# A hybrid SSD and pooling layer: the output projection as seven block products over all 16 k tiles, and the plain form of the seven in the down projection

## The chip, the cores and the metric

The kernel runs on one core of a Trainium2 chip. The metric is the device time of one execution in microseconds (us), given as the median of several runs; one execution of it is recorded by the profiler. Engines: PE multiplies matrices (PEld loads its weights), DVE and ACT work on vectors, POOL is the GpSimd engine, and SP issues DMAs. Each engine takes its own instructions in the order in which they stand in its queue. POOL and ACT issue DMAs too, and such an issue stands in their queues as an instruction.

## The reference

One decoder layer over 1024 prompt tokens and 8 sample tokens (1032 columns), all in float32. What matters here:

```
hn   = rmsnorm(x, norm1_w)
proj = hn @ w_in                          # z, xBC, dt, v
y_ssd, y_pool = ssd(...), pool_mixer(v)   # 1536 + 512 channels
x  = x + concat([y_ssd, y_pool]) @ w_out  # 2048 -> 1024
hn = rmsnorm(x, norm2_w)
u  = causal_dwconv(hn @ w_up)             # 1024 -> 2 * 2816
x  = x + (silu(gate) * val) @ w_down      # 2816 -> 1024
y  = rmsnorm(x, final_norm_w)
```

The states of the convolutions, the scan and the pooling are outputs as well; the change does not touch them.

## The kernel before

All activations lie feature-major: a k tile is 128 features by 1032 tokens. To keep float32 accuracy, every operand is split into a high part (ACT copies it to a shorter float type) and a low part (DVE subtracts that copy from the original): `split` does it for the moving operands (lines 208 to 212), `weight_parts` for weights of up to 512 columns (134 to 142). A product of two tiles is then three matmuls (high x high, high x low, low x high) which add up in PSUM.

The program's stages in the recorded execution: input projection, scan and pooling end at 516 us, the output projection `w_out` runs to 717.7, the up projection to 1165, the down projection and the final norm to the end at 1406.

**The output projection** (`w_out`, line 894). Two parts of six SSD tiles each run over the eight outputs n in chunks of 344 tokens, 18 matmuls a chunk; DVE adds each chunk from PSUM onto the residual `x2` (line 920). The four pooling tiles come last, one half of the tokens after the other, in columns of 258 (`w_out_end`, line 956); their evacuations (line 969) complete an output, ACT squares it (976), POOL or a product with ones adds the squares up, and `rn` gives the norm of the up projection's input. Weights come by SP straight from DRAM, in pieces of 384 or 512 columns. The last pooling group (`pool_tile`, line 834) ends beside the first SSD rows: its window sums on DVE and POOL, a split, nine products with the weights `pw`, and an evacuation to `pf`.

Twelve times in `w_out`, `down_sums` (line 1240) is called. It loads four blocks of the down weights, forms their sums for four of the seven products of the down projection with POOL, and puts them into DRAM.

**The down projection** (`down`, line 1305). The matrix product is cut into 2 x 2 blocks (even and odd output tiles by two halves of the 22 k tiles; two halves of 516 tokens) and done as seven products instead of eight. The form used here is that with shared sums: p1's result is kept as `U` (two tiles in SBUF), p6 and p7 are added to it, and U is added onto blocks of the residual (`sink`, line 1327). The operand sums of the seven are formed in the up projection by `spill` (line 1224) and written to DRAM (`td`); for each product POOL loads 11 operands (`down_ops`, line 1263, DMA at 1270), ACT and DVE split them. Each product has four outputs m, two quarters q of 258 tokens, and 11 k tiles in three pieces of 4, 4 and 3 (`PIECES`). p1, p2 and p4 take their weights straight from `wdn`, the others from the sums in DRAM. The first product runs over pieces outside and m inside, so that it holds eight PSUM banks; the last runs quarter by quarter with the final norm, whose first half (`norm_half`) is started within it.

The order on each engine is fixed when the program is built. Instructions are emitted in program order, with some moved behind a named instruction (`behind`) and with priorities by a scheduler, so code that stands later in the source can stand earlier on an engine's queue.

Of the kernel before, what the change touches and what calls it, by code (L numbers as in the profile page):

```python
# [10 lines left out]
F32 = mybir.dt.float32  # L11
# [7 lines left out]
P = 128  # L19
# [22 lines left out]
DOWN = ("p1", "p2", "p5", "p6", "p7", "p4", "p3")  # L42
DIRECT = {"p1": (0, 0), "p2": (0, 1), "p4": (1, 1)}
ROW = {"p1": 0, "p2": 1, "p3": 2, "p5": 3, "p7": 4, "p6": 5, "p4": 6}
# [31 lines left out]
class Kernel:  # L76
# [657 lines left out]
    def project(self):  # L734
# [5 lines left out]
        with ExitStack() as outer:  # L740
# [5 lines left out]
            with self.banks(g=4, pT=2, pY=1, pM=1) as self.ps, tc.tile_pool(name="mix", bufs=1) as self.ph:  # L746

                self.tags = {"bc": ("v", 2), "st": ("mh", 1), "stt": ("ml", 1), "dx": ("vs", 2)}
                for i in range(7, 12):
                    self.sample_tile(1, i)  # L750
                    self.gate_tile(16 + i, i, None)
                self.pool_groups()
# [133 lines left out]
    def pool_groups(self):  # L886
        pf = {}
        for g in (3, 2, 1, 0):
            pf[g] = self.pool_tile(g, g == 0)
        self.hn = None  # L890
        self.w_out([pf[g] for g in range(4)])


    def w_out(self, pf):
        nc, d = self.nc, self.d
        ops = []
        for i in range(6):
            o = (self.bigt(F32R, TOK, "yh"), self.bigt(F32R, TOK, "yl"))
            self.split(self.xs[i][:, :TOK], *o)
            ops.append(o)  # L900
        self.x2 = []
        for n in range(KT):
            t = self.bigt(F32, TOK, "x2")
            nc.sync.dma_start(t, d["xT"][:, n])
            self.x2.append(t)

        self.sums = {}
        todo = [(m, s) for s in range(len(PIECES)) for m in range(KT // 2)]

        def part(ops, k0, first, done=None):  # L910
            for n in range(KT):
                if first <= n < first + 6:
                    self.down_sums(len(todo), *todo.pop(0))
                nk = len(ops)
                ws = self.load_tile(d["wout"][n][:, k0 * P : (k0 + nk) * P], nk, 3 if nk == 6 else 4)
                t = self.x2[n]

                def evac(c, ps):
                    tc_ = t[:, c * CH : (c + 1) * CH]
                    nc.vector.tensor_tensor(out=tc_, in0=tc_, in1=ps, op=ALU.add)  # L920

                (self.gemm_k if n == KT - 1 else self.gemm)(ws, ops, evac)
                if done is not None:
                    done(n)
# [688 lines left out]
```

## Time and profile before

| | us |
|---|---|
| median of 3 runs (1406.89 to 1411.45) | 1409.72 |
| the profiled execution's own time | 1407.76 |
| its span, first to last instruction | 1406.0 |
| PE busy in the span | 1360.4 |
| output projection, 516.0 to 717.7 | 201.7 |
| up projection, 717.7 to 1165 | 447.3 |
| down projection and end, 1165 to 1406 | 241.0 |

How to read the lines that follow. A row of a group has line, engine, operation, output and inputs by name, shapes and count, then busy time in us and mean ns of one, then the idle time of that engine just before and what ended it. A matmul's mean is its latency; consecutive ones overlap, so what one costs on PE is a stretch without idle time divided by the number in it. A row of the windows has the stretch, its length, then busy time and number of instructions for PE, PEld, DVE, ACT and POOL, then the granted TensorE clock, the DMA share and GB/s. A row of the timeline has start, duration, engine, line and operation. A row of DMA issues has queue, count, KB of each, and the median us from issue to landing.

### The profile page before, as it was taken

The numbers are of one execution on the slowest core, as the hardware profiler recorded it, in microseconds if no ns is written. First come the engines' busy times: TensorE is split into PE (matmuls) and PEld (weight loads), VectorE is DVE, ScalarE is ACT, GpSimd is POOL, SyncE is SP. The second block draws the span as 40 slices with busy tenths as digits, with TensorE's granted clock in tenths as the row PEclk, the third lists the DMA queues.
The fourth block names the chain that finished last, engine by engine and source line by source line (L and its number), as shares of the span: only waits on it lengthen the run. The fifth ranks groups of instructions, "written<-read, shape, count | busy, mean of one in ns | idle before, by whom it ended". The sixth has DMA issues, their size and how long they took to land. (4 is left out here: it accounts for less than half of the span.)

```text
span 1406.0 us, 26779 instructions
## 1 busy us (share of the span) xinstructions
PE 1360.4 (97%) x10360; PEld 1312.9 (93%) x10360; DVE 991.2 (70%) x1453; ACT 700.6 (50%) x1408; POOL 561.5 (40%) x704
## 2 busy tenths in 40 slices
PE   8999999979999999999979999999999999999997
PEld 7799879968799999899979999999999999999997
DVE  6575898669865684844689877777776787567743
ACT  6346774546644451311456545554554465444452
POOL 4233465888668305774222212212222224214122
PEclk9999999989999999999999999999999999999999
DMA  6031235243331256675477877777777769657513
GB/s 248 1 108 38 93 118 168 81 142 116 94 104 62 74 192 209 214 253 178 152 204 148 210 205 193 187 207 183 185 187 201 196 207 328 225 185 235 180 55 121
DMA packets 117820, 228.09 MB, mean 162 GB/s; under 512 B 19884, under 2 KB 37116, under 8 KB 117692
## 3 DMA queue, kind: packets, MB, share of 16 engines
q1 hardware_dynamic: 73772, 130.21, 29.3%
q0 software_dynamic: 27056, 70.22, 19.8%
q10 hardware_dynamic: 16864, 25.95, 5.6%
q8 instruction: 81, 1.33, 0.4%
q14 instruction: 47, 0.39, 0.1%
HBM read 169.64 MB, written 45.15 MB: 153 GB/s over the span
## 5 line engine op out<-in xcount | busy, mean ns | idle before, releaser
L1118 PE MATMUL g<-op,wop 128*128 128x258 f32 x3696 | 446.9, 283 | 4.3 <-DVE op L1048 1.6
L1118 PEld LDWEIGHTS g<-op,wop 128*128 128x128 f32 x3696 | 445.3, 189 | 5.6 <-DVE op L1048 2.0
L140 ACT ACTIVATE wop<-raw 128x512 fp32r<-128x512 f32 (+1 forms) x208 | 125.9, 608 | 231.2 <-PE g L161 139.7
L1300 PE MATMUL g<-op,wop 128*128 128x258 f32 x1848 | 224.9, 283 | 1.6 <-ACT op L210 0.9
L159 PE MATMUL g<-hh,wop 128*128 128x344 f32 x696 | 226.1, 325 | 0.0
L160 PE MATMUL g<-hl,wop 128*128 128x344 f32 x696 | 225.3, 324 | 0.0
L1300 PEld LDWEIGHTS g<-op,wop 128*128 128x128 f32 x1848 | 222.5, 189 | 2.7 <-ACT op L210 1.1
L161 PE MATMUL g<-hh,wop 128*128 128x344 f32 x696 | 224.8, 323 | 0.0
L141 DVE TENSOR_TENSOR wop<-raw,wop 128x512 fp32r<-128x512 f32 (+1 forms) x186 | 159.7, 862 | 83.3 <-ACT wop L140 81.5
L140 ACT ACTIVATE wop<-s 128x512 fp32r<-128x512 f32 (+1 forms) x136 | 83.6, 620 | 137.6 <-PE g L1300 51.9
L1098 POOL DMA_DIRECT2D s<-s x44 | 37.7, 857 | 249.8 <-DVE wop L141 89.2
L159 PEld LDWEIGHTS g<-hh,wop 128*128 128x128 f32 x696 | 132.2, 190 | 1.2 <-issue 1.1
L161 PEld LDWEIGHTS g<-hh,wop 128*128 128x128 f32 x696 | 132.1, 190 | 1.2 <-issue 1.2
L160 PEld LDWEIGHTS g<-hl,wop 128*128 128x128 f32 x696 | 132.1, 190 | 0.5 <-issue 0.4
L1200 DVE SCALAR_TENSOR_TENSOR acc<-u,cst,acc 128x1048 f32<-128x1048 f32 x88 | 115.2, 1309 | 12.2 <-ACT acc L1198 10.6
L141 DVE TENSOR_TENSOR wop<-s,wop 128x512 fp32r<-128x512 f32 (+1 forms) x136 | 92.1, 682 | 36.5 <-ACT wop L140 34.1
L1178 DVE TENSOR_TENSOR u<-u,g 128x258 f32<-128x258 f32 (+2 forms) x176 | 58.0, 354 | 72.2 <-PE g L1118 67.6
L1175 ACT ACTIVATE u<-g 128x258 f32<-128x258 f32 (+2 forms) x220 | 69.6, 340 | 71.2 <-PE g L1118 71.2
L160 PE MATMUL g<-yl,wop 128*128 128x344 f32 x288 | 93.4, 325 | 3.2 <-DVE yl L211 3.2
L161 PE MATMUL g<-yh,wop 128*128 128x344 f32 x288 | 93.0, 323 | 0.0
L159 PE MATMUL g<-yh,wop 128*128 128x344 f32 x288 | 92.9, 323 | 0.0
L1270 POOL DMA_DIRECT2D g<-td x77 | 41.2, 539 | 123.1 <-DVE op L211 70.2
(276 smaller groups left out, 2333.9 us busy)
## 6 DMA issues: line engine op xcount, KB each, us to landing
s<-wup SPq DMA_DIRECT2D x88, 256.0 KB, 3.2
g<-td POOLq DMA_DIRECT2D x77, 258.0 KB, 4.5
raw<-wup SPq DMA_DIRECT2D x66, 256.0 KB, 4.1
raw<-win SPq DMA_DIRECT2D x58, 256.0 KB, 2.7
mix<-acd SPq DMA_DIRECT2D x16, 768.0 KB, 4.5
td<-acc ACTq DMA_DIRECT2D x22, 516.0 KB, 6.1
s<-wup POOLq DMA_DIRECT2D x44, 256.0 KB, 5.3
s<-s POOLq DMA_DIRECT2D x44, 256.0 KB, 3.9
```

The source lines that it names most:

```text
L140: self.nc.scalar.activation(hi, raw[:, :w], AF.Copy)
L141: lo_eng.tensor_tensor(out=lo, in0=raw[:, :w], in1=hi.bitcast(F32), op=ALU.subtract)
L159: nc.tensor.matmul(ps[:, :n], wh, xh[:, sl], start=(first and k == 0), stop=False)
L160: nc.tensor.matmul(ps[:, :n], wh, xl[:, sl], start=False, stop=False)
L161: nc.tensor.matmul(ps[:, :n], wl, xh[:, sl], start=False, stop=(final and k == last))
L1098: nc.gpsimd.dma_start(t, raw[acc] if acc in raw else w[acc][j], accum_op=ALU.add)
L1118: nc.tensor.matmul(out, a, b, start=(p in OPENS and j == 1), stop=(j == 12), skip_group_check=True)
L1175: a = nc.scalar.activation(out, ps[:, s], AF.Copy, scale=-1.0 if p in ("p5", "p4") else 1.0)
L1178: nc.vector.tensor_tensor(out=out, in0=out, in1=ps[:, s], op=op)
L1200: nc.vector.scalar_tensor_tensor(out=acc, in0=u[:, k : k + FW], scalar=self.c("fw", 3 * n + k), in1=acc, op0=ALU.mult, op1=ALU.add)
L1270: self.loaded = self.nc.gpsimd.dma_start(st[:, j], self.td[i + j][ROW[p]]).ins
L1300: self.pe = nc.tensor.matmul(out, a, b, start=(s == 0 and i == 0 and j == 0), stop=(s == len(PIECES) - 1 and i == nk - 1 and j == 2),).ins
```

## The change

**Output projection.** `w_out` now treats all 16 k tiles at once as 2 x 2 blocks: even and odd output tiles; the k tiles in pairs, of which the first of each pair is x and the second y (`block`); two halves a, b of the tokens. Seven products n2, n4, n1, n5, n7, n3, n6 run over 8 k tiles, 4 outputs m and 2 quarters of 258 tokens. `SIDE` lists the operand sum of each, `SRC` the weight sum, `INTO` where the result is added: `into` adds a PSUM quarter onto one or two blocks of the residual. No sum of results is kept. The operand sums of n4 are formed by DVE, those of n1, n7, n3 and n6 by POOL, the last three in place. The weights of n4 and n3 are blocks of w_out; those of n2, n5, n6 and n7 are loaded by SP in 512 KB and the second block is added to them by a DMA on POOL's queue; for n1 POOL subtracts. The first product, n2, runs over two halves of k outside and m inside and holds eight PSUM banks. The squares for the norm are added by POOL as outputs are completed in n5, n7, n3 and n6; the rows of w_out are permuted on the host.

**Down projection.** The same seven products in the order n4, n2, n1, n5, n7, n3, n6 with the same `SRC` and `INTO`; `U` goes, and with it ACT's copies and DVE's adds of it. `down_sums` goes: for n2, n1, n5, n7 and n6 each piece of weights is two loads by SP and one sum on POOL (`down_weights`). `spill` forms five operand sums instead of four. `norm_half` of the first token half moves from the last product to n3.

```diff
+OUT = ("n2", "n4", "n1", "n5", "n7", "n3", "n6")
+SIDE = {
+    "n2": ("xa",), "n4": ("ya", "xa", ALU.subtract), "n1": ("xa", "yb", ALU.add), "n5": ("yb",),
+    "n7": ("ya", "yb", ALU.add), "n3": ("xb", "yb", ALU.subtract), "n6": ("xa", "xb", ALU.add),
+}
+SRC = {
+    "n1": ((0, 0), (1, 1), ALU.subtract), "n2": ((1, 0), (1, 1), ALU.add), "n3": ((0, 0), None, None),
+    "n4": ((1, 1), None, None), "n5": ((0, 0), (0, 1), ALU.add), "n6": ((1, 0), (0, 0), ALU.add),
+    "n7": ((0, 1), (1, 1), ALU.add),
+}
+INTO = {
+    "n1": ((0, 0, ALU.add), (1, 1, ALU.subtract)), "n2": ((1, 0, ALU.add), (1, 1, ALU.subtract)),
+    "n3": ((0, 1, ALU.add), (1, 1, ALU.subtract)), "n4": ((1, 0, ALU.add), (0, 0, ALU.subtract)),
+    "n5": ((0, 0, ALU.subtract), (0, 1, ALU.add)), "n6": ((1, 1, ALU.add),), "n7": ((0, 0, ALU.add),),
+}
...
     def w_out(self, pf):
...
+        def sums(p):
+
+            if len(SIDE[p]) == 1:
+                sides[p] = [block(i, SIDE[p][0]) for i in range(NP)]
+                return
+            s0, s1, op = SIDE[p]
+            eng = nc.vector if p == "n4" else nc.gpsimd
...
+        def weights(p, m):
...
+            nc.sync.dma_start(t, src(one, 0, 2))
+            if op == ALU.add:
+                nc.gpsimd.dma_start(t, src(two, 0, 2), accum_op=op)
+            out = [t[:, :512], t[:, 512:]]
+            if op != ALU.add:
+                for s in range(2):
+                    more = self.raw(False)
+                    nc.sync.dma_start(more, src(two, s))
+                    nc.gpsimd.tensor_tensor(out=out[s], in0=out[s], in1=more, op=op)
+            return out
...
+            if k == 0:
+                sums(after)
+                side(after, 0, 3, more)
+                for s in range(2):
+                    for m in range(NM):
+                        both = self.weight_parts(raws[m][s], 512, nc.vector)
+                        for q in range(2):
+                            self.piece(ps[m][q][:, :TQ], both, ops[4 * s : 4 * s + 4], q, s == 0, s == 1)
+                            if s == 1:
+                                self.into(self.x2, p, m, q, ps[m][q][:, :TQ])
...
     def down_weights(self, p, m, s, pool=None):
...
+        one, two, op = SRC[p]
+        raw = self.raw(two is not None)[:, :w]
+        nc.sync.dma_start(raw, block(*one))
+        if two is not None:
+            more = self.raw(False)[:, :w]
+            nc.sync.dma_start(more, block(*two))
+            nc.gpsimd.tensor_tensor(out=raw, in0=raw, in1=more, op=op)
+        return self.weight_parts(raw, w, nc.vector, pool)
...
+    def into(self, x2, p, m, q, ps):
+
+        ins = None
+        for i, t, op in INTO[p]:
+            out = x2[2 * m + i][:, t * TH + q * TQ : t * TH + (q + 1) * TQ]
+            ins = self.nc.vector.tensor_tensor(out=out, in0=out, in1=ps, op=op).ins
+        return ins
```

What this moves, at three places. First PE's queue where the output projection starts. `hh` and `hl` are the operands of the input projection, `mh` and `ml` those of the pooling groups (the last group has the numbers 5261 and 5262), `yh` and `yl` the split SSD rows. Before:

```order
L161 MATMUL pY_5153<-mh_5133,pw_5139 128x344
L161 MATMUL g_5174<-hh_94,wop_5165 128x344
L159 MATMUL g_5355<-yh_5286,wop_5347 128x344
L160 MATMUL g_5355<-yl_5287,wop_5347 128x344
L161 MATMUL g_5355<-yh_5286,wop_5347 128x344
L159 MATMUL g_5355<-yh_5290,wop_5347 128x344
```

And the same place now; the `op` tiles are n2's operands and g_5343 to g_5347 its PSUM banks.

```order
L179 MATMUL g_5174<-hh_94,wop_5165 128x344
L177 MATMUL pT_5271<-mh_5261,pw_5267 128x344
L177 MATMUL pM_5276<-mh_5261,pw_5267 128x344
L177 MATMUL pY_5281<-mh_5261,pw_5267 128x344
L178 MATMUL pT_5271<-ml_5262,pw_5267 128x344
L179 MATMUL pT_5271<-mh_5261,pw_5267 128x344
L178 MATMUL pM_5276<-ml_5262,pw_5267 128x344
L179 MATMUL pM_5276<-mh_5261,pw_5267 128x344
L178 MATMUL pY_5281<-ml_5262,pw_5267 128x344
L179 MATMUL pY_5281<-mh_5261,pw_5267 128x344
L1371 MATMUL g_5343<-op_5291,wop_5372 128x258 x3
L1371 MATMUL g_5343<-op_5294,wop_5372 128x258 x3
```

The last pooling group's products stood among the SSD rows' work (the first of them 61 rows behind the first of w_out's); now all nine stand ahead of it.

Second, POOL's queue at the same time. `sa` and `sb` are the pooling groups' window sums, `ds` and `sd` the down weights' sums. Before:

```order
L862 TENSOR_TENSOR sb_5125<-sb_5125,cst 128x3
L862 TENSOR_TENSOR sa_5253<-sa_5253,cst 128x1
L1253 TENSOR_TENSOR ds_5327<-ds_5327 128x512
L1253 TENSOR_TENSOR ds_5416<-ds_5416 128x512
L1255 DMA sd_5334<-ds_5327 128x512
```

And now; `s_5315`, `s_5318`, `s_5321` and `s_5324` are the weights of n2 for m = 0, 1, 2 and 3 (the DMAs add the second block), and the sums onto `xs` are operands of n7, formed in place of rows that n4's differences on DVE read first.

```order
L884 TENSOR_TENSOR sb_5125<-sb_5125,cst 128x3
L977 DMA s_5315<-wout 128x1024
L884 TENSOR_TENSOR sa_5253<-sa_5253,cst 128x1
L977 DMA s_5318<-wout 128x1024
L958 TENSOR_TENSOR xs_1228<-xs_1228 128x516
L977 DMA s_5324<-wout 128x1024
L958 TENSOR_TENSOR xs_2087<-xs_2087 128x516
L958 TENSOR_TENSOR xs_832<-xs_832 128x516
L958 TENSOR_TENSOR xs_1030<-xs_1030 128x516
L977 DMA s_5321<-wout 128x1024
```

POOL's work for the down weights is gone from here, and weights and operands of the output projection alternate in its queue.

Third, POOL's queue where the last product of the down projection begins; `td` are the operands in DRAM, `g` the tiles they are loaded into, `ssq` the sums of squares. Before, the last product's loads, and what follows:

```order
L1270 DMA g_15620<-td_12099 128x516
L1270 DMA g_15620<-td_12616 128x516
L1270 DMA g_15629<-td_13151 128x516
L1367 TENSOR_TENSOR ssq_13232<-ssq_13232,sq_15301 128x516
L1367 TENSOR_TENSOR ssq_13232<-ssq_13232,sq_15392 128x516
```

And now, where sq_15812 is the square of the last output of n3, the product before the last:

```order
L1340 DMA g_15842<-td_11643 128x516
L1416 TENSOR_TENSOR ssq_13296<-ssq_13296,sq_15722 128x516
L1359 TENSOR_TENSOR s_15975<-s_15975,raw_15977 128x384
L1359 TENSOR_TENSOR s_15998<-s_15998,raw_16000 128x512
L1359 TENSOR_TENSOR s_16018<-s_16018,raw_16020 128x512
L1359 TENSOR_TENSOR s_16038<-s_16038,raw_16040 128x384
L1416 TENSOR_TENSOR ssq_13296<-ssq_13296,sq_15812 128x516
L1340 DMA g_15851<-td_12161 128x516
L1340 DMA g_15851<-td_12679 128x516
L1359 TENSOR_TENSOR s_16061<-s_16061,raw_16063 128x512
L1359 TENSOR_TENSOR s_16081<-s_16081,raw_16083 128x512
L1340 DMA g_15860<-td_13215 128x516
```

The loads of the ninth to eleventh operand of the last product stood ahead of all the squares; now they stand behind weight sums and behind the square of the product before.

375 lines of the change are left out of this document (181 added, 194 removed).

## The prediction

> **What bounds the kernel now.** I read the granted clock and the engines' busy time first, then the chain that ended last, then three windows cut where the program's stages meet (output projection, up projection, down projection).
>
> ```profile
> core 0: 1406.0 us, clock 0.984
> PE 1360.4 (97%) x10360; PEld 1312.9 (93%) x10360; DVE 991.2 (70%) x1453; ACT 700.6 (50%) x1408; POOL 561.5 (40%) x704
> ...
> PE 46%; DMA 0%; ACT 0%; DVE 0%; DVEq 0%; issue 0%; ACTq 0%
> ```
>
> PE is busy for 97% of the span at a full clock, and nothing else has a share of the chain: time is matmul time plus PE's gaps. The windows (span, then PE, PEld, DVE, ACT, POOL busy with instruction counts, clock, DMA share, GB/s) say where gaps are.
>
> ```profile
> 516.00:717.70 201.70, 193.80 (x1283) 191.25 (x1281) 120.99 (x161) 58.03 (x104) 100.67 (x107) 0.97 0.65 209
> 717.70:1165.00 447.30, 443.02 (x3671) 441.80 (x3670) 342.25 (x541) 240.87 (x509) 108.66 (x180) 1.00 0.77 196
> 1165.00:1406.00 241.00, 230.94 (x1901) 228.90 (x1900) 150.15 (x269) 111.05 (x211) 61.85 (x97) 0.99 0.56 186
> ```
>
> The change touches the first and third. Both are PE-bound; POOL has half of its time free in the first, three quarters in the third. Undisturbed stretches give the price of one matmul, fuller ones the gaps:
>
> ```profile
> 580.00:600.00 20.00, 16.82 (x89) 16.09 (x88) 19.90 (x15) 7.97 (x10) 14.46 (x14) 0.83 0.55 170
> 600.00:660.00 60.00, 60.00 (x384) 60.00 (x383) 24.84 (x39) 7.94 (x15) 38.05 (x47) 1.00 0.69 225
> 690.00:700.00 10.00, 10.00 (x86) 10.00 (x85) 8.98 (x14) 6.43 (x11) 3.63 (x3) 1.00 0.31 102
> 708.00:718.00 10.00, 5.75 (x22) 4.37 (x20) 7.45 (x13) 4.96 (x16) 0.60 (x1) 0.73 0.53 161
> ...
> 1300.00:1360.00 60.00, 60.00 (x504) 60.00 (x503) 38.03 (x73) 27.85 (x52) 12.29 (x16) 1.00 0.40 129
> ```
>
> A matmul of 344 columns takes 60/384 = 0.156 us, one of 258 columns 10/86 = 0.117 to 60/504 = 0.119 us.
>
> **The change, output projection: PE's work.** Before: 864 matmuls of 344 (12 k tiles, 8 outputs, 3 chunks, 3 terms) and 384 of 258 (4 k tiles, 8 outputs, 4 quarters, 3 terms): 134.8 + 45.2 = 180.0 us. With about 7 us of ones and pooling products that leaves some 15 us of gaps and slow clock in 201.7: about 6 at 580 to 600, 7 at 708 to 718. After: 7 products x 8 k tiles x 4 m x 2 quarters x 3 = 1344 matmuls of 258 = 157.9 us, with 5.5 for ones and pooling 163.4. PE gives up 38 us of occupied or lost time if nothing new waits. Five losses are new.
>
> *Start, 7 us (5 to 10).* The timeline at the stage's start, DVE and ACT:
>
> ```profile
> 517.12 0.48 ACT L847 ACTIVATE v<-g 128x336 f32<-128x336 f32 x1
> ...
> 517.62 1.24 DVE L858 TENSOR_TENSOR sa<-v 128x1038 f32<-128x1038 f32 x1 [0.77 <-ACT v L847]
> ...
> 519.49 1.23 DVE L864 SCALAR_TENSOR_TENSOR sb<-sa,v 128x1024 f32<-128x1024 f32 x1
> ...
> 522.80 1.23 DVE L211 TENSOR_TENSOR ml<-sb,mh 128x1032 fp32r<-128x1032 f32 x1
> ```
>
> This is the last pooling group: its values leave PSUM at 517.1 and its operand's low half is there at 524.0. Before, PE ran SSD rows of w_out meanwhile. Now PE's order has that group's nine products ahead of the first product of w_out, whose second half needs the pooled rows as well. PE is out of work at 516 and starts w_out at about 524.5, having done 1.4 us: 7 lost. ACT's copy of the first weight also stands ahead of the group's evacuations, so a late weight adds to it.
>
> *Weights of m = 1, 2 and 3, 14.5 us (8 to 18).* The later weights of n2 are sums of two blocks, made by an accumulating DMA of 512 KB on POOL's queue, which now stands behind the pooling group's head (519.5) and, for m = 3 and m = 2, behind one and four operand sums on POOL that themselves wait for n4's differences on DVE. Prices:
>
> ```profile
> s<-wup POOLq DMA_DIRECT2D x44, 256.0 KB, 5.3
> ...
> x<-xT SPq DMA_DIRECT2D x8, 516.0 KB, 6.6
> L1253 POOL TENSOR_TENSOR ds<-ds,ds 128x512 f32<-128x512 f32 x24 | 33.3, 1409 | 3.0 <-DMA ds<-wdn 2.8
> ...
> L211 DVE TENSOR_TENSOR op<-x,op 128x516 fp32r<-128x516 f32 x9 | 5.8, 682 | 0.0
> ```
>
> No row has an accumulate of 512 KB; between one of 256 KB (5.3) and two of them (10.6) I take 7, nearest the 516 KB load. Weight m = 1: issue 520, landing 527, two halves of a split 1.3: PE, free at 524.5 + 2.8, waits 1.5. Then DVE's difference 0.7, POOL's sum 1.4, issue 0.9, three sums 4.3, issue 0.9, landing 7, split 1.3: 16.5 from 528.5 to m = 2, of which m = 1's work covers 3: 13 lost. Until then PE has nothing else in its queue.
>
> *Slow clock after these gaps, 4 us (2 to 6).* At 708 to 718, after gaps, the granted clock is 0.73. The Trainium skill, "TensorE: Matmul & The Clock Gate", section "What's actually happening", says an idle window of about 3.4 us halves the clock until as long a busy one; the 0.73 agrees. By it the two gaps cost half of 3.4 us each, 3.4 in all, beside the 4 taken from the row.
>
> *DVE and POOL beside each other in n4 and n1, 7 us (2 to 12).* The same DVE instruction alone, and beside POOL's sums:
>
> ```profile
> 509.08 1.23 DVE L211 TENSOR_TENSOR yl<-xs,yh 128x1032 fp32r<-128x1032 f32 x1 [0.59 <-ACT yh L210]
> ...
> 578.19 11.96 DVE L211 TENSOR_TENSOR yl<-xs,yh 128x1032 fp32r<-128x1032 f32 x4
> ...
> 579.17 4.54 POOL L1253 TENSOR_TENSOR ds<-ds,ds 128x512 f32<-128x512 f32 x2
> ```
>
> It takes 2.99 instead of 1.23 us. New POOL sums in the stage: 32 of operands, 8 of weights, some 12 of squares, 52 x 1.41 = 73 us, 40 of them placed within three products of 22.6 us each. DVE's share of one product is 8 weight splits, 8 operand splits (16 x 0.68 = 10.9) and 16 PSUM adds (x 0.42 = 6.7): 17.6 of 22.6, with little room for blocking. I take a little over half of a gap such as that at 580 to 600 (6 us) for each of n4 and n1.
>
> *End, 1 us.* The second half's norm no longer needs eight late squares; 708 to 718 lost about 5, now about 1.
>
> The stage: 163.4 + 7 + 14.5 + 4 + 7 + 1 = 196.9, against 201.7: **-5** (-18 to +8).
>
> **Up projection.** The spill of operands gets a fifth DVE difference (11 x 0.7 us), in a stage where DVE has 105 us free: +0.5 (0 to 1).
>
> **Down projection.** PE's 1848 matmuls stay. The 48 DRAM sums go (their time lay on POOL beside w_out). In their place each of five products has 12 sums on POOL. Rows of this stage:
>
> ```profile
> L211 DVE TENSOR_TENSOR op<-g,op 128x516 fp32r<-128x516 f32 x73 | 51.3, 723 | 3.0 <-ACT op L210 2.9
> ...
> L1270 POOL DMA_DIRECT2D g<-td x61 | 32.6, 538 | 109.7 <-DVE op L211 70.2 <-PE g L1300 20.6 <-issue 5.9
> L141 DVE TENSOR_TENSOR wop<-s,wop 128x512 fp32r<-128x512 f32 x32 | 23.1, 728 | 13.5 <-ACT wop L140 13.3
> L1333 DVE TENSOR_TENSOR x<-x,g 128x258 f32<-128x258 f32 x40 | 15.8, 419 | 23.7 <-PE g L1300 23.7
> ...
> L1367 POOL TENSOR_TENSOR ssq<-ssq,sq 128x516 f32<-128x516 f32 x10 | 13.2, 1331 | 32.3 <-ACT sq L1366 25.6 <-ACT ssq L1363 6.5
> ```
>
> A product is 264 matmuls = 31.4 us on PE. POOL: 12 sums of at most 1.41 = 16, 11 operand loads of 0.54 = 6, in three products four adds of squares of 1.33 = 5: 22 to 27. DVE: 23 splits of 0.72 = 16.6 and 16 adds = 6.7: 23. Both fit. But POOL's queue is in order, and the loads of the next product's operands (L1270 before) now stand among the weight sums; those wait for weight buffers (seven), which free as PE proceeds. The median load lands 4.5 us after issue, and the tenth and eleventh operand are wanted 5.7 us into a product. For the last operand of n1, n5 and n7, issued a few us into its product after the last sums, I take 3 us of PE gap each (0 to 6): 9. At n6, the last product, the loads of operands 9 to 11 stand behind the add of n3's last square, and the eleventh behind two sums more:
>
> ```profile
> g<-td POOLq DMA_DIRECT2D x77, 258.0 KB, 4.5
> ```
>
> From n3's end: PSUM add 0.4, square 0.6, add 1.3, issue 0.5 twice, landing 4.5, split 1.3: 9 us to the ninth and tenth operand, 12 to the eleventh. PE has some 5 us of other work: 7 lost (5 to 14). Before, this boundary lost 2.7:
>
> ```profile
> 1363.22 0.02 issue
> ...
> 1365.88 2.55 PE g L1300 x19
> ```
>
> So +4.5. The sum for the stage: 9 + 4.5 = **+13.5** (-1 to +31).
>
> **Sum.** On the profiled execution's own 1407.76 us (span 1406.0 and 1.76 around it): 1407.8 - 5 + 0.5 + 13.5 = 1416.8, say **1417**. The three runs have a median of 1409.7, 2 us above the profiled one; I let that stand within the range. About 0.3% (4.2 us) is what a measurement of this kernel tells from no change.
>
> **Rivals.** *The waits are short, faster.* If the weights of m = 2 and 3 come with m = 1's (POOL's four sums wait for nothing, or DMAs land in 5), the 14.5 falls to 4, the slow clock to 2, the port's 7 to 3; if buffers let the down loads run ahead, the 13.5 falls to 3. Then 1407.8 - 21.5 + 0.5 + 3 = 1390. For it: 38 us of PE time are given up for certain, POOL is free for 60% of the whole span. Against it: the fixed order on POOL's queue. It decides if the gap between m = 1 and m = 2 is under 4 us and no down boundary shows over 1 us. Chance 0.34. *Gains and losses cancel, within 0.3%.* Half of both: 1405.5 to 1414. Chance 0.12. *POOL and DVE pace the down products.* If a POOL sum stops DVE's two-input operations altogether, DVE's 23 us and POOL's 16 of sums add to 39 for each of five products, against 31.4 on PE: +38, less some 10 where adds from PSUM go on beside the sums, and the boundaries' 9 lie within it: 1407.8 - 5 + 0.5 + 28 + 4.5 = 1436. The Trainium skill, "SBUF — State Buffer", section "Who interferes with whom", has that rule: DVE with two SBUF inputs and a GpSimd instruction that reads SBUF lock each other out for whole instructions, while one SBUF input does not contend. The 2.99 for 1.23 us agrees with it. By it the sum would be this rival's 1436. Against it: the four splits beside POOL also ended when POOL paused. Chance 0.12.
>
> **How the numbers follow.** The forecast has 0.42, and with the rival above it slower 0.54; same 0.12; faster 0.34. The range takes in the fast rival's 1390 with 6 us below it (the start's and the norm's bounds) and, above, the pacing one's 1436: 1384 to 1440. The forecast's own range is 1414 to 1428.
>
> **What would show it.** In the profile after: PE idle from the end of the in-projection to the first matmul of n2 for 7 us, then after some 48 matmuls of it about 13 us; 1344 matmuls of 258 before the up projection; at n6 a PE gap of about 7 us that ends at an operand split; DVE splits of over 1.2 us where POOL sums. It is wrong if the output stage ends within 185 us, if the down stage has no gap at its boundaries, or if the clock's drops after gaps cost more than the gaps.

## The result, and the profile after

| | us |
|---|---|
| before, median of 4 runs (1404.06 to 1411.45) | 1408.31 |
| after, median of 4 runs (1473.65 to 1480.61) | 1476.27 |
| ratio after to before | 1.0488, 95% interval 1.0448 to 1.0528 |
| the profiled execution of after, its span | 1473.65, 1471.9 |

The change makes the kernel 4.9% slower. The forecast was 1417 in a range of 1384 to 1440: the side was right, the size outside the range. The page of after, the same lines as before:

```profile
core 0: 1471.9 us, clock 0.962
PE 1363.2 (93%) x10448; PEld 1308.8 (89%) x10448; DVE 1074.0 (73%) x1544; ACT 722.0 (49%) x1448; POOL 629.9 (43%) x726
...
PE 37%; DMA 5%; DVE 3%; POOL 1%; issue 1%; ACT 1%; DVEq 0%; POOLq 0%; SPq 0%; ACTq 0%
```

PE is idle for 109 us instead of 46, its clock has fallen, and transfers, DVE and POOL have come onto the chain that ends last. To place this I cut both spans at the same events: the last matmul of the input projection, the first of the up projection, its last, the last of the down projection's products, and the end.

| us | input projection, scan, pooling | output projection | up | down products | tail |
|---|---|---|---|---|---|
| before | 515.7 | 202.0 | 452.5 | 225.5 | 10.3 |
| after | 513.7 | 207.7 | 454.3 | 283.4 | 12.8 |
| difference | -2.0 | +5.7 | +1.8 | +57.9 | +2.5 |

The first column differs by up to 15 us between executions of kernels whose code is the same there (508 to 523), so below I compare the stages of single runs, not their totals. A stage differs between runs as well: in two of the runs below (`w_raw`, `h_down`) the code of the down projection is that of after, and its products took 274.5 and 278.5 us for 283.4. So a single profile that shows this stage less than about 9 us below after's does not show a gain. Two windows of after (span; PE, PEld, DVE, ACT, POOL busy; clock, DMA share, GB/s), the output projection and the down products:

```profile
513.90:721.40 207.50, 176.73 (x1371) 172.41 (x1370) 166.44 (x235) 83.96 (x157) 93.58 (x68) 0.93 0.60 163
1175.90:1459.40 283.50, 243.09 (x1851) 236.53 (x1850) 182.17 (x270) 106.05 (x195) 140.87 (x158) 0.92 0.62 202
```

The second row is the finding: no engine but PE is busy for more than two thirds of it, and yet PE is idle for 40.4 us of 283.5. The timeline of PE in after's down projection gives the larger gaps (in brackets the idle time before a stretch and what ended it):

```profile
1213.62 40.06 PE L1371 MATMUL g<-op,wop 128*128 128x258 f32 x316 [10.99 <-ACT op L228]
...
1265.28 4.73 PE L1371 MATMUL g<-op,wop 128*128 128x258 f32 x24 [3.18 <-ACT op L228]
...
1399.72 9.62 PE L1371 MATMUL g<-op,wop 128*128 128x258 f32 x56 [3.36 <-DVE wop L159]
...
1419.90 2.22 PE L1371 MATMUL g<-op,wop 128*128 128x258 f32 x6 [6.27 <-ACT op L228]
```

The waits of the stage (waiter, what it waited for: sum, count, longest):

```profile
ACT op L228 <- DMA g<-td: 86.9, 31, 8.1
POOL s L1359 <- DMA raw<-wdn: 45.9, 4, 30.1
POOL s L1359 <- DMA s<-wdn: 39.4, 12, 9.8
PE g L1371 <- ACT op L228: 28.9, 9, 11.0
PE g L1371 <- DVE wop L159: 5.6, 4, 3.4
PE g L1371 <- ACT wop L158: 4.8, 3, 1.9
```

PE waits for operands (28.9 us) more than for weights (10.4); the operands wait for their loads from `td`; and POOL, which issues those loads, waits 45.9 us for the second blocks of weight sums (four times, at n2 and at n6, the two products that follow one with direct weights) and 39.4 us for first blocks (twelve times). The largest gap is near n4's end: by the count PE has done 240 of n4's 264 matmuls, and the last 24 need n4's eleventh operand, whose load the program issues behind eight of n2's. The timelines of POOL and of SP's queue there:

```profile
1196.81 4.28 POOL L1359 TENSOR_TENSOR s<-s,raw 128x512 f32<-128x512 f32 x3 [30.14 <-DMA raw<-wdn]
1201.04 1.09 POOL L1340 DMA_DIRECT2D g<-td  x2
1202.15 4.65 POOL L1359 TENSOR_TENSOR s<-s,raw 128x512 f32<-128x512 f32 x4
1206.75 1.61 POOL L1340 DMA_DIRECT2D g<-td  x3
```

```profile
1152.44 10.91 SPq L1355 DMA_DIRECT2D s<-wdn  x4
...
1164.84 24.60 SPq L1355 DMA_DIRECT2D raw<-wdn  x9
...
1194.07 13.09 SPq L1358 DMA_DIRECT2D raw<-wdn  x11
```

SP has the first blocks of n2 (`s`) on their way by 1163. Then come n4's direct weights (`raw`, L1355), which fill the four `raw` buffers, and only from 1194 the second blocks of n2 (L1358), which use the same four. So POOL stands for 30.1 us at the first sum of n2's weights. Behind it in its queue, among the sums, stand four of n2's operand loads and then the load of n4's last operand, the third of the three at 1206.75. The chain that ended last goes exactly that way:

```profile
1199.69 3.21 DMA raw<-wdn
1202.93 1.30 POOL s L1359 x2
...
1206.75 1.08 POOL g L1340 x2
1207.83 5.09 DMA g<-td
1212.94 0.64 ACT op L228
1213.62 2.53 PE g L1371 x10
```

In the output projection, timeline of PE: the start, and the wait within n2.

```profile
521.53 0.66 PE L177 MATMUL pT<-mh,pw 128*128 128x344 f32 x1 [7.52 <-ACT mh L228]
...
543.66 32.06 PE L1371 MATMUL g<-op,wop 128*128 128x258 f32 x242 [12.55 <-ACT wop L158]
```

These two are the gaps of 7 and 13 us that were forecast. After them come n4 (from 563), n1 (588), n5 (619) and n7 (646), in windows of 20 us and one of 100:

```profile
560.00:580.00 20.00, 19.66 (x160) 19.23 (x160) 20.00 (x29) 5.78 (x10) 15.52 (x11) 1.00 0.26 67
580.00:600.00 20.00, 15.21 (x109) 14.07 (x107) 20.00 (x21) 8.23 (x15) 19.49 (x14) 0.92 0.61 188
...
560.00:660.00 100.00, 89.88 (x703) 87.29 (x703) 89.77 (x125) 37.34 (x66) 58.12 (x42) 0.97 0.60 149
```

DVE is busy without a pause from 560 to 600, beside a busy POOL; PE loses 10.1 us from 560 to 660.

### The profile page after: what moved, and what is told of

Its sections match the earlier page's. It is cut to its first block, busy times and chain, and to the rows that moved or that the text cites. A ratio compares the mean times of both kernels' runs of the same rounds, so it can differ in the third digit from the quotient of the medians.

```text
span 1471.9 us, 27093 instructions
## 1 busy us (share of the span) xinstructions
PE 1363.2 (93%) x10448; PEld 1308.8 (89%) x10448; DVE 1074.0 (73%) x1544; ACT 722.0 (49%) x1448; POOL 629.9 (43%) x726
## 3 DMA queue, kind: packets, MB, share of 16 engines
q8 instruction: 82, 1.34, 0.4%
## 5 line engine op out<-in xcount | busy, mean ns | idle before, releaser
L1371 PE MATMUL g<-op,wop 128*128 128x258 f32 x3192 | 414.3, 292 | 63.2 <-ACT op L228 29.9
L1371 PEld LDWEIGHTS g<-op,wop 128*128 128x128 f32 x3192 | 403.4, 196 | 72.7 <-ACT op L228 32.2
L1210 PE MATMUL g<-op,wop 128*128 128x258 f32 x3696 | 447.4, 283 | 5.5 <-ACT op L1135 5.1
L1210 PEld LDWEIGHTS g<-op,wop 128*128 128x128 f32 x3696 | 446.0, 190 | 6.5 <-ACT op L1135 5.5
L178 PE MATMUL g<-hl,wop 128*128 128x344 f32 x696 | 225.5, 324 | 0.0
L158 ACT ACTIVATE wop<-s 128x512 fp32r<-128x512 f32 x188 | 113.8, 617 | 196.7 <-PE g L1210 48.9
L159 DVE TENSOR_TENSOR wop<-s,wop 128x512 fp32r<-128x512 f32 x188 | 158.2, 854 | 42.5 <-ACT wop L158 40.4
L158 ACT ACTIVATE wop<-raw 128x512 fp32r<-128x512 f32 (+1 forms) x164 | 101.7, 625 | 112.4 <-PE g L1371 44.5
L159 DVE TENSOR_TENSOR wop<-raw,wop 128x512 fp32r<-128x512 f32 (+1 forms) x142 | 115.8, 820 | 52.8 <-ACT wop L158 52.4
L1359 POOL TENSOR_TENSOR s<-s,raw 128x512 f32<-128x512 f32 (+1 forms) x60 | 80.0, 1347 | 108.8 <-DMA raw<-wdn 45.9
L229 DVE TENSOR_TENSOR op<-g,op 128x516 fp32r<-128x516 f32 x77 | 69.6, 920 | 57.5 <-ACT op L228 57.2
L1270 DVE TENSOR_TENSOR u<-u,g 128x258 f32<-128x258 f32 (+2 forms) x176 | 58.3, 355 | 67.0 <-PE g L1210 64.3
L1380 DVE TENSOR_TENSOR x<-x,g 128x258 f32<-128x258 f32 x192 | 70.5, 416 | 31.7 <-PE g L1371 31.4
L228 ACT ACTIVATE op<-g 128x516 fp32r<-128x516 f32 x77 | 47.5, 629 | 88.3 <-DMA g<-td 86.9
```

Of the source, the lines that this page charges most:

```text
L158: self.nc.scalar.activation(hi, raw[:, :w], AF.Copy)
L159: lo_eng.tensor_tensor(out=lo, in0=raw[:, :w], in1=hi.bitcast(F32), op=ALU.subtract)
L178: nc.tensor.matmul(ps[:, :n], wh, xl[:, sl], start=False, stop=False)
L229: (lo_eng or nc.vector).tensor_tensor(out=lo, in0=src, in1=hi.bitcast(F32), op=ALU.subtract)
L1210: nc.tensor.matmul(out, a, b, start=(p in OPENS and j == 1), stop=(j == 12), skip_group_check=True)
L1359: nc.gpsimd.tensor_tensor(out=raw, in0=raw, in1=more, op=op)
```

## The experiments

My theory after the result: in the down projection the sums on POOL sit in one queue with the operand loads, and their inputs share buffers and SP's queue with the direct weights. Rivals: DVE and POOL stop each other (the pacing rival on record); the extra 256 KB loads alone; the operands' queue alone; the output projection's new order leaking into the later stages.

**Order of POOL's queue, and the raw buffers.** `d_order` puts every operand load that stands earlier in the program ahead of each sum; `d_raws` lets direct weights use the seven `s` buffers too.

```diff
+            with self.behind(self.loaded):                      # d_order
+                nc.gpsimd.tensor_tensor(out=raw, in0=raw, in1=more, op=op)
-        raw = self.raw(two is not None)[:, :w]
+        raw = self.raw(True)[:, :w]                             # d_raws
```

> Order alone, in the down projection: each weight sum on POOL is placed behind the last operand load of its own product, so that no operand load waits in POOL's queue behind a sum of its own product. Theory Q (POOL's queue: operand loads stand behind weight sums that wait for buffers which only PE's progress frees): PE's gaps in the down stage fall from 40 us to at most 15, and with them the slow clock; total about 1435, 35 to 45 below the changed kernel's 1474. Rival P (POOL's sums and DVE's two-input operations lock each other out): the same sums and splits are left, so the time stays within 10 us of 1474. Rival B (the second block of each weight sum overloads the DMAs): the same, within 10 us of 1474.

> Buffers alone: the direct weights of n4 and n3 in the down projection go into the seven buffers of the first blocks, so that the four raw buffers hold second blocks only. Theory Q, with the raw buffers as the place where the first sum of n2 waited 30 us: the 11 us gap at the boundary from n4 to n2 falls below 3, the other boundaries keep most of theirs (some 25 us); total about 1460. Rivals P and B: no change, 1474 within 5.

`d_order`: 1463.09 us, ratio to before 1.0395 (1.0348 to 1.0443); down products 269.9, 13.5 less than after. Its four runs (1461.12 to 1464.80) all lie below after's four, so a gain is shown, but of 13 us and not of the 40 expected. The gaps did not go, they changed sides, from operands to weights. PE's timeline in `d_order`:

```profile
1218.05 32.91 PE L1372 MATMUL g<-op,wop 128*128 128x258 f32 x260 [5.14 <-DVE wop L159]
...
1259.42 1.23 PE L1372 MATMUL g<-op,wop 128*128 128x258 f32 x4 [8.46 <-ACT wop L158]
```

`d_raws`: 1482.67 us, down 287.4, and the gap near n4's end is still 9.69 us, where under 3 was expected: sharing the other buffers in place of these is no better.

**No sums, and no arithmetic.** `d_nosum` drops the second block and the sum in `down_weights`; `d_loads` drops the sum only.

```diff
         if two is not None:                                     # d_nosum: all of these
             more = self.raw(False)[:, :w]
             nc.sync.dma_start(more, block(*two))
-            nc.gpsimd.tensor_tensor(out=raw, in0=raw, in1=more, op=op)   # d_loads: this one
```

> Leaves out the second block of every weight sum in the down projection, its load and the sum on POOL (so the weights of n2, n1, n5, n7 and n6 are one block only). Lower bound of all theories: the down stage back to about 232 us, total about 1415. By Q the order-only run comes within 20 us of this one; by P and B it stays 45 to 60 above.

> Leaves out the sum on POOL but keeps both loads of every weight piece in the down projection, in the same buffers (the weights are one block only). Rival B (the second blocks overload the DMAs): as slow as the changed kernel, 1460 or more. Q and P: what remains of POOL's work there is operand loads, so 1422 within 6, as with the second block left out altogether.

`d_nosum`: 1422.71 us, down 230.4; from n2's fifth matmul to the middle of n3 PE runs in one piece:

```profile
1208.70 141.97 PE L1367 MATMUL g<-op,wop 128*128 128x258 f32 x1184 [0.63 <-DVE wop L159]
```

1184 matmuls at 0.120 us. So 53 of the 58 us belong to the sums and their loads; splits, operand loads and additions from PSUM keep up without them. `d_loads`: 1449.78 us, down 251.1, half way, with a single large gap at another place: within n2, behind 144 of its 264 matmuls, and it ends at a weight and not at an operand. SP sends 29 second blocks one after another, the DMA share is 0.97, and n2's remaining first blocks stand behind them (PE's timeline, a window, SP's queue):

```profile
1242.81 20.48 PE L1370 MATMUL g<-op,wop 128*128 128x258 f32 x144 [11.40 <-ACT wop L158]
```

```profile
1200.00:1231.00 31.00, 31.00 (x259) 30.83 (x258) 18.50 (x38) 11.71 (x22) 9.10 (x17) 1.00 0.97 335
```

```profile
1202.48 34.60 SPq L1358 DMA_DIRECT2D raw<-wdn  x29
```

With no sum to free them one by one, the second blocks go ahead of the first blocks that are wanted, so this run prices the loads in an order of its own and is no clean half of the cost.

**The weights of the output projection.** `w_raw` loads the two blocks of m = 2 and 3 apart and adds them on POOL ahead of the operand sums.

```diff
-        raws = [weights(OUT[0], m) for m in range(NM)]
+        raws = [weights(OUT[0], m) for m in range(2)] + [[], []]
+        one, two, op = SRC[OUT[0]]
+        for s in range(2):
+            for m in (2, 3):
...
+                last = nc.gpsimd.tensor_tensor(out=w[0], in0=w[0], in1=w[1], op=op).ins
```

> Output projection alone: the weights of n2 for m = 2 and 3 are loaded as two blocks into the raw buffers and summed by POOL ahead of its operand sums, in place of accumulating DMAs behind them. The prediction's chain (DVE difference, POOL sum, DMA, three sums, DMA): PE's 12.6 us gap after m = 1 falls below 3 and the slow clock behind it goes, total 1474 - 14 = 1460. Rival: POOL and DVE beside each other set the pace there, and the gap moves into n4 and n1: total 1470 to 1476.

1460.41 us; the stage took 201.4 instead of 207.7. PE's timeline in `w_raw`:

```profile
544.01 17.10 PE L1383 MATMUL g<-op,wop 128*128 128x258 f32 x128 [3.55 <-DVE wop L159]
...
621.87 50.25 PE L1383 MATMUL g<-op,wop 128*128 128x258 f32 x398 [5.82 <-DVE op L229]
```

The 12.55 us gap has become 3.55, and a new one of 5.82 stands in n5, behind DVE; PE's idle time in the stage fell from 30.8 to 24.9 us. The total is the 1460 that was expected, but by luck: the output projection gave 6 of the 14 us, and the down projection, which this edit leaves alone, was 9 shorter. Two more runs with this edit, `v1` and `v2` below, have 198.9 and 197.4 here, where the runs with after's output projection have 205.5 to 211.0; by these the edit is worth about 9.

**The queue of the operand loads, and accumulating DMAs.** `d_tdact` issues the `td` loads on ACT, `d_acc` makes the additive sums by DMA on POOL's queue, `d_accact` both.

```diff
-                self.loaded = self.nc.gpsimd.dma_start(st[:, j], self.td[i + j][ROW[p]]).ins
+                self.nc.scalar.dma_start(st[:, j], self.td[i + j][ROW[p]])    # d_tdact
+        if two is not None and op == ALU.add:                                # d_acc
+            nc.gpsimd.dma_start(raw, block(*two), accum_op=op)
```

> The down projection's operand loads are issued on ACT's queue instead of POOL's; sums and everything else as in the changed kernel. The order-only run moved PE's gaps from operands (30 us) to weights (45 us), so theory Q now reads: POOL's one queue holds two streams that each wait for the other's buffers, and either order makes one late. With the loads off that queue neither stands behind the other: PE's gaps in the down stage under 15 us, total about 1440. Rival P (POOL's sums and DVE's two-input operations pace each other): the sums stay, so 1465 or more. A third outcome, 1450 to 1465: the loads now hold ACT's queue, and the halves of weights behind them are late.

> The weight sums of n2, n5, n7 and n6 in the down projection are made by accumulating DMAs on POOL's queue (no second buffer, no POOL arithmetic); n1 keeps its sums. It takes away the lock and the sharing of the raw buffers, but each accumulating DMA still stands in POOL's queue ahead of operand loads and waits there for its first block. If buffers and lock were the cause: down stage 240 to 250, total about 1440. If the order of POOL's queue alone was: 270 or more, total 1460 or more.

> Both at once in the down projection: the sums of n2, n5, n7 and n6 by accumulating DMAs on POOL's queue, and the operand loads on ACT's queue. It differs from the run with accumulating DMAs (down stage 275) in the loads' queue alone, and from the run with loads on ACT's queue (271) in the sums alone. Theory Q2 (two streams, each waiting for buffers that the other's progress frees, on one in-order queue; and the second blocks sharing the raw buffers with n4's direct weights): with both couplings gone the down stage falls to 235 to 245, total about 1437. Rival R (each stream is late by itself, whatever the queue: POOL's sums, ACT's loads): 260 or more, total 1458 or more.

Down products 271.3, 274.9 and 274.6 (runs of 1467.45, 1472.84 and 1464.67 us). That is 9 to 12 us below after, but 274.5 and 278.5 are there without any edit of the stage, so none of the three is shown to gain, and theory Q2 has failed: with both couplings gone the stage is not at 235 to 245. In `d_acc` the gap near n4's end is gone, since n2's second blocks no longer pass through the raw buffers; in its place stand gaps of 5.82, 4.59 and 6.24 us in n1, n5 and n6. In `d_tdact` it is still 10.34: there ACT issues the loads two at a time, each pair behind splits that wait for an earlier pair. So taking the loads off POOL's queue is no repair by itself.

**Sums on DVE.** `d_dve` forms the sums on DVE (`nc.vector` for `nc.gpsimd` in the line above), so that POOL has no arithmetic there but the squares; `d_dveact` has the `td` loads on ACT as well.

> The weight sums of the down projection are made by DVE instead of POOL; loads, buffers and order rules as in the changed kernel. POOL's queue then holds operand loads and squares only, and no POOL sum meets DVE's two-input operations. DVE's own work grows by 60 x 0.7 = 42 us in a stage of some 280, within which it was busy 200. Theory Q (POOL's queue and the lock together; the raw buffers apart, whose share the run with loads alone gave as some 20 us): down stage 250 to 255 against 283, total about 1445. Rival (DVE in turn becomes the bound, as its queue is in order and a sum now waits there for its second block): 1470 or more.

> The down projection's weight sums on DVE and its operand loads on ACT's queue. POOL has squares only: no lock, and operand loads no longer share a queue with anything that waits for weights on POOL. The run with the sums on DVE alone had a down stage of 265. If what is left of the 58 us is operand loads waiting in a queue: 245 or less, total about 1438. If it is the extra step in the supply of weights (two loads and a sum, in order, before each split) and the DMAs' crowding at n4 and n2: 258 to 268, total 1452 to 1462.

Down 265.0 and 274.0 (1458.26 and 1461.99 us); the second lies outside both ranges of its expectation, and loads on ACT's queue again bring nothing. In `d_dve` DVE's operand split takes 725 ns again; in after it takes 943. The groups by form, first of after, then of `d_dve`:

```profile
L229 DVE TENSOR_TENSOR op<-g,op 128x516 fp32r<-128x516 f32 x70 | 65.0, 943 | 57.5 <-ACT op L228 57.2
L159 DVE TENSOR_TENSOR wop<-s,wop 128x512 fp32r<-128x512 f32 x40 | 40.1, 1024 | 4.6 <-ACT wop L158 4.6
L1380 DVE TENSOR_TENSOR x<-x,g 128x258 f32<-128x258 f32 x96 | 35.0, 418 | 26.7 <-PE g L1371 26.7
```

```profile
L229 DVE TENSOR_TENSOR op<-g,op 128x516 fp32r<-128x516 f32 x72 | 50.9, 725 | 1.9 <-ACT op L228 1.9
```

So POOL's sums do lengthen DVE's splits of two SBUF inputs, by 30% to 40%, and leave its adds from PSUM as they were (418; 419 before). But 70 splits by 0.22 and 40 by 0.3 us are 27 us of DVE, which was idle for 101 in this stage. The gap near n4's end stayed without POOL's arithmetic (PE's timeline, then DVE's):

```profile
1219.41 39.70 PE L1371 MATMUL g<-op,wop 128*128 128x258 f32 x316 [12.79 <-DVE op L229]
```

```profile
1215.63 0.69 DVE L1359 TENSOR_TENSOR s<-s,raw 128x512 f32<-128x512 f32 x1 [1.31 <-DMA raw<-wdn]
1216.24 3.12 DVE L229 TENSOR_TENSOR op<-g,op 128x516 fp32r<-128x516 f32 x5
```

POOL issued the load of n4's last operand at 1193.29 here, but the sums now stand in DVE's queue ahead of five operand splits, and SP still sends their second blocks from 1197.09 on. The wait follows the second blocks, on whichever engine the sums are.

**Buffers and a queue of their own.** `d_own` gives the second blocks two buffers of their own and ACT's queue; `d_owndve` has the sums on DVE besides.

```diff
-            more = self.raw(False)[:, :w]
-            nc.sync.dma_start(more, block(*two))
+            more = self.spool.tile([P, 512], F32, tag="second", name=self.nm("more"), bufs=2)[:, :w]
+            nc.scalar.dma_start(more, block(*two))
```

> The second blocks of the down projection's weights get two buffers of their own and are loaded on ACT's queue, so that neither the raw buffers nor SP's queue is shared with them; sums on POOL and operand loads on its queue as in the changed kernel. If sharing the raw buffers and SP's queue makes the 11 us gap at the boundary from n4 to n2: that gap under 4 and a down stage of 268 to 275. If crowded DMAs make it (with the second loads alone it stood there too, at a DMA share of 0.94): 280 to 290.

> Second blocks in two buffers of their own on ACT's queue (23 us alone) and the sums on DVE (18 us alone). If the first removes the sharing of buffers and of SP's queue, and the second the lock and the sums that operand loads wait behind on POOL's queue, the two are separate and add: down stage 283 - 41 = 242, within 6, total about 1433. If they are two sides of one wait: 255 to 262, total 1448 or more.

`d_own`: 1446.95 us, down 260.4, 23 less than after: the largest gain of a single edit that still forms the sums in the stage. PE's timeline at n2's start, where n4 has ended without a gap, and at n6:

```profile
1202.59 34.78 PE L1371 MATMUL g<-op,wop 128*128 128x258 f32 x285 [0.63 <-DVE wop L159]
...
1392.49 0.58 PE L1371 MATMUL g<-op,wop 128*128 128x258 f32 x1 [4.32 <-ACT op L228]
```

The 10.99 is gone; the first gap now is the 0.63 behind n2's fourth matmul, which the kernel without sums has too. It shows that the shared path of the second blocks made that gap; whether buffers or SP's order weigh more isn't separated, since the edit moves both. (In `d_loads` the gap did not stand there too, as this expectation has it, but within n2.) `d_owndve`: 1445.44 us, down 256.1. The gains of 23 and 18 do not add up: the two are sides of one wait, as the second branch of its expectation has it.

**The sums formed earlier, in DRAM.** `d_dram` forms those of n2, n5, n7 and n6 during the input projection, by 16 copies of 704 KB on SP and 16 accumulating DMAs on POOL; n1 stays. `v1` is `d_dram` with `w_raw`.

```diff
+        if (p, m) in self.sums:
+            nc.sync.dma_start(raw, self.sums[p, m][:, k0 * P : (k0 + nk) * P])
+            return self.weight_parts(raw, w, nc.vector, pool)
```

> The weight sums of n2, n5, n7 and n6 of the down projection are formed in DRAM during the input projection, by 16 copies of 704 KB on SP's queue and 16 accumulating DMAs on POOL's; the down projection loads them as single pieces, and POOL sums for n1 alone. Q and P: the gaps at n2, n5, n7 and n6 fall to those of the run without sums, n1 keeps some 5 us: down stage about 238 us, total about 1428, plus whatever the early DMAs cost the input projection (0 to 6).

> The run before it together with the raw-buffer weights of n2 in the output projection (14 us saved alone): the two lie in different stages and add, so about 1413; 1405 or less would beat both kernels.

Down 239.1 and 241.3 (1456.08 and 1439.92 us; `v1` to before 1.0217, 1.0186 to 1.0249): with four of five products' sums out of the stage 44 of the 58 us are gone, as expected. The totals are 28 and 27 us above those expected, since much is given back at once: the input projection ends at 539.2 and 533.3, where the runs without these DMAs have 508 to 523. Its wait of PE for the scan in `d_dram`, 11.8 us against 4.5 in after:

```profile
PE pM L585 <- DVE h L630: 11.8, 3, 7.3
```

**The halves apart, and the best of both.** `h_down` has before's output projection without `down_sums`, and after's down projection. `h_best` adds `d_accact` to it, `h_owndve` adds `d_owndve`; `v2` is `w_raw` with `d_accact`.

```diff
-                with self.banks(g=8) as self.ps:
-                    self.w_out(pf)
+        self.w_out([pf[g] for g in range(4)])     # 12 + 4 k tiles as before, no down_sums in it
```

> The down projection's half of the change alone: the output projection of before without the sums of down weights, then up and down of the changed kernel. If the stages are independent: the output stage 201.8 less the 6 us gap at 580 to 600 = 195, down stage 283 as in the changed kernel, total 1472 - 12 = 1460. If what the new output projection leaves behind sets the down stage's order or timing, the down stage differs from 283 by over 10.

> The output projection of before without the sums of down weights, and the down projection of the run above. Output stage 195.5 as in the down-only run; down stage by Q2 235 to 245 where before had 225.5: total 1408 - 6 + 10 to 20 = 1412 to 1422; 1404 or less would beat both kernels. By R 1435 or more.

> The changed kernel with both repairs: raw-buffer weights of n2 in the output projection (output stage 199 to 201) and the down projection of the first of these runs: by Q2 a total of 1425 to 1430, by R 1448 or more.

> The same down projection behind the output projection of before without its sums of down weights (output stage 195.6). If the two repairs add: 1452 - 41 = 1411; if they are one: 1428. 1403 or less would beat the kernel before.

`h_down`: 1452.48 us; output projection 195.7, down 278.5, so 53 of the 58 us are lost behind before's output projection as well, and the rival that the new one leaks into later stages fell. The old output projection without the sums that it carried is 12 us faster than the new one. In `h_down` DVE beside an idle POOL has room there and PE never stops:

```profile
580.00:600.00 20.00, 20.00 (x129) 20.00 (x128) 12.71 (x20) 6.75 (x10) 0.00 (x0) 1.00 0.14 41
```

`h_best` 1445.86 us (ratio to before 1.026, 1.0201 to 1.0318), `v2` 1450.67, `h_owndve` 1428.92 (1.0152, 1.011 to 1.0193; the 1428 of "if they are one"), the fastest of those that form all the sums, with stages of 195.3 and 252.2. `h_best` and `v2` have the down products of `d_accact` again, at 270.1 and 273.0. No version that I tried beats the kernel before.

## Why the prediction was right in side and wrong in size

**Output projection, -5 forecast, +5.7 measured.** The start (7; 7.52) and the weights of m = 1, 2 and 3 (14.5; 12.55) came out as forecast, the first by the steps given, the second partly by luck. The timelines of POOL and ACT there:

```profile
519.38 0.89 POOL L977 DMA_DIRECT2D s<-wout  x1 [0.31 <-issue]
...
528.64 0.87 POOL L977 DMA_DIRECT2D s<-wout  x1
...
534.31 0.86 POOL L977 DMA_DIRECT2D s<-wout  x1
```

```profile
542.97 2.19 ACT L158 ACTIVATE wop<-s 128x512 fp32r<-128x512 f32 x4 [9.68 <-DMA s<-wout]
```

The 512 KB accumulate of 534.31 landed at about 542.9, 8.6 us after issue and not 7, but it was issued 1.5 us before the 535.8 of the forecast's steps, and m = 1, landed 5.6 us after issue, cost no wait: the errors cancel. "DVE and POOL beside each other in n4 and n1, 7 us" is 10.1 from 560 to 660, but at other places: 0.3 in n4, 5.1 in n1 and 4.7 in n5 and n7. Idle time in all is 207.5 - 176.7 = 30.8 us, forecast 7 + 14.5 + 7 + 1 = 29.5. Mis-sized are the term of 4 us for the slow clock and the price of the work: PE is busy for 176.7 us with work priced at 163.4, 13.3 more. In three stretches the granted clock is 0.50 (518.1 to 524.9, 535.2 to 548.8, 596.6 to 603.4); PE is busy for 14.3 us in them, so the slow clock cost 7.2. Another 3 are an estimate of mine: 1344 matmuls at the 0.120 us of `d_nosum`'s long piece instead of 0.1175. The rest is open.

**Up projection, +0.5; +1.8.** The variants show 452.6 to 455.8 there; what makes the difference is open.

**Down projection, +13.5 forecast, +57.9 measured: the step that failed.** It is the one of the shared queue: "the loads of the next product's operands (L1270 before) now stand among the weight sums; those wait for weight buffers (seven), which free as PE proceeds", with "3 us of PE gap each (0 to 6): 9" for n1, n5 and n7. The mechanism is there: POOL's sums wait 39.4 us for first blocks, and n1, n5 and n7 have gaps of some 14 us in all for the 9. Four things in the price were not right:

- I followed the sums' first blocks (seven `s` buffers) and not their second ones. These come through the four `raw` buffers and SP's queue, behind n4's direct weights. The load of n4's last operand behind n2's first sums was given no price at all; it lost 11.0 us and shows as POOL's wait of 30.1. `d_own` removes that gap.
- The gaps elsewhere were larger and more: the end of n3 has one of 3.36 us, n6 one of 6.27 and four of under 2, 14.7 in all against 7; in the whole stage PE is idle for 40.4 us, 1.6 before (the window below).
- "Before, this boundary lost 2.7" reads the chain that ended last, where other engines' work stands between 1363.22 and 1365.88; PE itself was idle for 0.74 us there, so the forecast took off 2 us too much.
- "Slow clock after these gaps" was a term of the output projection and of no other stage. PE is busy for 243.1 us of the 283.5 with 1851 matmuls; before, 223.8 for the same number. So 39 us of new gaps brought 19 us more of busy time, and the two make the 58. In five stretches (44 us) the granted clock is 0.50, and PE is busy for 29.4 us in them: 14.7 of the 19 are the slow clock.

A window of before, cut at its last product matmul, for that comparison:

```profile
1165.00:1390.40 225.40, 223.77 (x1851) 222.65 (x1851) 146.34 (x264) 108.92 (x206) 60.16 (x96) 1.00 0.58 194
```

The Trainium skill, "TensorE: Matmul & The Clock Gate", section "What's actually happening", has the mechanism that idle windows halve the clock until PE has been busy again. Behind the gap of 10.99 us that agrees: 19 matmuls in 4.10 us at a clock of 0.50, and then 35 in 4.00 at 1.00 (two windows of after).

```profile
1213.70:1217.80 4.10, 4.10 (x19) 4.10 (x20) 2.22 (x6) 0.92 (x2) 1.36 (x3) 0.50 1.03 399
1218.00:1222.00 4.00, 4.00 (x35) 3.98 (x34) 4.00 (x11) 1.58 (x4) 0.15 (x1) 1.00 0.59 175
```

But the granted clock also fell to 0.50 at 1323.7, behind two gaps of 1.52 and 1.34 us; in the 3.4 us before, PE had been busy for 0.77. So short gaps close to each other were enough here.

What stays open: 260.4 of `d_own`, 256.1 of `d_owndve` and 252.2 of the same stage in `h_owndve` are still 22 to 30 us above the kernel without sums. Neither order, buffers, queue nor engine, each changed alone or in pairs, removes that rest. By `d_nosum` it belongs to the second blocks and their sums; which link of the way from two loads over a sum to a split makes it, no run settles.

**The rivals.** The fast one fell: neither of its conditions held (12.55 us between m = 1 and m = 2 for under 4; 10.99 in the down stage for none over 1). So did the one in which gains and losses cancel. The pacing one (1436) came nearest, and for the wrong reason: that POOL's sums slow DVE's splits is shown (943 for 725 ns), but DVE had idle time left, `d_acc` with POOL sums for n1 alone still took 274.9, and `d_dve` without any 265.0. It also priced only DVE's and POOL's busy times, as I did: 27 us of POOL and 23 of DVE in a product of 31 do fit, and the stage failed on the order in which they come.

## What to carry to other kernels

For a step that moves into a PE-bound stage, adding up busy times of the engines says only that it could fit: list for every new instruction each buffer and queue that its inputs need, who holds these when it is due, and what stands behind it on its engine. Price a gap of PE at about one and a half times its length where gaps come often, since the clock falls with them: 58 us for 39 in after's down products, 44 for 35 in `d_order`'s. An early sum in DRAM that "costs POOL time" in another stage may be cheap there: before, it cost 6 us of the output projection (202.0 against 195.7 without it), in the down projection it cost over 50. Before reading a gain off a stage of one profile, see how far that stage moves in runs whose code there is the same: here by 9 us.

## What I had not expected of the hardware

A 512 KB accumulating DMA into SBUF took 7.9 us from issue to landing (the median of 15 in after; 5.6 and 8.6 are the two above), for 5.3 of one of 256 KB, and 0.87 us of POOL to issue. Beside POOL's float32 sums DVE's splits were longer by a third to two thirds (725 to 943 ns in after, 1215 in `d_order`), but never its adds from PSUM (418 ns). And 32 DMAs of 704 KB within DRAM were placed in the input projection, whose DMA share was about 0.3 from 100 to 500 us: in the two runs with them it ended at 533 and 539 us instead of 508 to 523.
